# Chunk-band attention layer: third query weight split ahead of the next keys, output copies in the head norm's ring, and sixteen sums moved from GpSimd to VectorE

## The chip, the cores and the metric

The kernel runs on one core of a Trainium2 chip. The metric is device microseconds of one execution, the median of several. The engines are named as the profile names them: PE (TensorE, matrix products; PEld is its weight load), DVE (VectorE), ACT (ScalarE), POOL (GpSimd) and SP (SyncE, which issues most DMAs; SPq is its queue).

## The reference

One inference step of a two-layer trunk over 1024 prompt frames and 8 sample groups of 16 frames, model width 1024. Layer 0 is an RWKV-7 time mixing with an FFN, layer 1 a band attention with an FFN. The change lies in layer 1:

```python
            q = rms_norm((h @ p['wb_q'][j]).reshape(bsz, t, H_B, HEAD_B), p['q_norm'][j])
            o = band_attention(q, k_all, v_all, pos0, k_hist.shape[1], p['rel_bias'][j], qb)
            out = o.reshape(bsz, t, d) @ p['wb_o'][j]
        x = x + gt_m[:, None, :] * out
        h = modulate(rms_norm(x, p['norm_ffn'][l]), sh_f, sc_f)
        x = x + gt_f[:, None, :] * swiglu(h, p['w_gate'][l], p['w_up'][l], p['w_down'][l])
...
    def block(i):                                   # band_attention, 64 queries each
        s = jnp.einsum('bqhd,bkhd->bhqk', q_b, k_b).astype(jnp.float32) * scale + bias[None]
        s = jnp.where(allowed[None, None], s, NEG_INF)
        p = jax.nn.softmax(s, axis=-1)
        return jnp.einsum('bhqk,bkhd->bqhd', p.astype(v_b.dtype), v_b)
```

There are 16 heads of 64; a prompt query sees its own chunk of 64 keys and the 8 chunks before it, a sample query 512 cached keys and its own 16. Queries and keys are normed by head (`q_norm`, `k_norm`).

## The kernel before

**Arithmetic.** Each float32 operand x of a product is split into a high part (`ACTIVATE`, ACT, line 272) and a low part x - high (`TENSOR_TENSOR`, DVE, line 273); `mm3` then issues three matrix products, all at line 143. So a weight is ready for PE when ACT has made its high half and, for the third product, DVE its low half. A weight matrix arrives as two blocks of 128x512 (`halves`, line 249 for the DMA), into raw slots and from there into `wh` tiles of a ring of three.

**Order of the work.** Instructions are written by Python generators, and then put in order on each engine by a scheduler that works from a model of the time; tiles come from pools, each tag a ring of a few buffers, and a tile waits for the last reader of the buffer it takes. `slot(1)` is one such ring, of 128x1024 tiles called `h` in the profile, used for raw weights, raw keys, queries and the splits of FFN inputs. Each engine runs its list in order.

**Stages.** After the keys and values of layer 1, `attention`'s queries for the first two pairs of heads (weights n = 0 and 1) are made with PE fully fed, ending about 2423 us. Then eight pairs of heads are worked through, n = 0 to 7, about 2423 to 2930 us:

- `pair(n)` asks for the keys and queries of the next pair (`kprep`: two DMAs from `out_kT`, line 1624, then a split of 128x1024; `qprep`: a DMA from `qT`, line 1631, then a split of 64x1024 in two parts), the values (`vf`, line 1740) and the bias rows of both heads (`bt`, line 1744, scaled on DVE at 1745).
- 16 tiles, for 8 blocks of 128 queries and two heads, run as a pipeline of four steps: scores on PE (`S<-h,h`) with bias and row minimum on DVE (1802); exponential on ACT (1803); the division on DVE (1805, 1806); transposes of P on PE (1811) and their copy `pts` on ACT (1812); then, for a pair of tiles, the output `O<-pts,vf`. Every second block, `heads_out` copies O (128x256) on DVE (1833) into a tile `o` and sends it to memory.
- Two sample groups per pair (`samples`, cache blocks `kc`, `vc`, queries `qsm`) stand among the tiles.
- As filler, `queries(n + 2)` makes the queries of the pair after the next: `head_steps` issues 24 products `acc<-h,wh` a step group, four groups for each weight, each closed by a head norm: ACT 1518 and 1522, a product `acc<-ht,cst` that sums squares, then `rsqrt2` (ACT 330 to 332, DVE 333, 334) and DVE 1526. Its tiles `ht` come from a ring of five.

Then `attproj` multiplies the outputs by `wo` (about 2931 to 3003 us), eight blocks of weights, adds the residual, and meanwhile makes the FFN's operands of the first half of the frames: `strassen_in` with c = 0 norms X, splits it, and makes sums of blocks (`comb`, line 1299, 128x256 each, 16 of them on POOL) which are split again. The last FFN begins about 3003 us, with the same for the other half (sums on DVE), and keeps PE full from about 3050 us to the end.

The lines that `attention`, `pair` and `attproj` share with the rest:

```python
        self.evt = lambda tag: self.pp.tile([128, 320], F32, tag=tag, ..., bufs={"xin": 2, "ht": 5}[tag])
        gp = gp or nc.gpsimd          # strassen_in(self, B, x, r, A, sh0, c, X, gp=None): engine of the sums
        self.split(t[1], t[2], raw)   # kprep: high part on ACT, low part on DVE
```

Of the kernel before, what the change touches and what calls it, by code (L numbers as in the profile page):

```python
# [8 lines left out]
F32 = mybir.dt.float32  # L9
F32R = mybir.dt.float32r  # L10
AF = mybir.ActivationFunctionType
ALU = mybir.AluOpType
# [133 lines left out]
class Trunk:  # L146
# [133 lines left out]

    def gemm(self, out, W, hi, lo, m=128):

        whi, wlo = W
        for k in range(8):
# [3 lines left out]

    def gemm_steps(self, out, W, hi, lo):

# [1275 lines left out]
    def kv(self, H, X, end):  # L1566
        nc = self.nc
        kn, qn = (self.cp.tile([128, 1], F32, name=n) for n in ("kn2", "qn2"))
        nc.vector.tensor_scalar(kn, self.P("kn", 0), -0.5, None, ALU.mult)
        nc.vector.tensor_scalar(qn, self.P("qn", 0), 0.5 * 0.125, None, ALU.mult)  # L1570
        self.qn = qn
        nw = 4
        W = [self.halves(self.a["wk"][n]) for n in range(nw)]
        for c in (1, 0):
            for n in range(nw):
                self.head(n, c, W[n], H, kn[:, 0:1], self.kT)
                for _ in range(3):
                    next(end, None)
            for _ in end:
                pass  # L1580
        for n in range(nw, 8):
            W = self.halves(self.a["wk"][n])
            for c in (1, 0):
                self.head(n, c, W, H, kn[:, 0:1], self.kT)
        self.HQ = {}
        Aq = self.gain("nm1", 56)
        for n in range(4):
            W = [h for u in range(2) for h in self.halves(self.a["wv"][n, u])]
            for c in range(2):
                for w in range((4, 5)[c]):  # L1590
                    ws = slice(w * 128, (w + 1) * 128)
                    pz = self.wide()[:, 0:256]
                    for k in range(8):
                        ks = slice(k % 2 * 256, (k % 2 + 1) * 256)
                        wh, wl = W[k // 2]
                        self.mm3(pz, H[c][0][k][:, ws], H[c][1][k][:, ws], wh[:, ks], wl[:, ks], k == 0, k == 7)
                    vt = self.ev("vt")[:, 0:256]
                    nc.scalar.activation(vt, pz, AF.Copy)
                    nc.sync.dma_start(self.o["v"][4 * c + w, :, n * 256:(n + 1) * 256], vt)
                if n == 3:  # L1600
                    self.HQ[c] = self.feats(c, F32R), self.feats(c, F32R)
                    for _ in self.normed_split(c, *X[c], Aq, 48, *self.HQ[c]):
                        pass
        self.KQ = {}
        for e in range(2):
            self.kprep(0, e)
        for n in range(2):
            if n:
                self.evt = lambda tag: self.slot(1)
            W = self.halves(self.a["wq"][n])  # L1610
            for c in range(2):
                self.head(n, c, W, self.HQ, qn[:, 0:1], self.qT)
            if n == 0:
                for e in range(2):
                    self.qprep(0, e)
# [18 lines left out]
    def attention(self, ctx):  # L1634
        nc, tc = self.nc, self.tc
        at = self.at = self.pp = self.wq = ctx.enter_context(tc.tile_pool(name="att", bufs=1, reuse_waits="tile"))
        self.hw = ("wh", "wl", 3)
        self.halfraw = lambda: self.slot(1)[:, :512]
        self.evt = lambda tag: self.pp.tile([128, 320], F32, tag=tag, name=self.nm(tag), bufs={"xin": 2, "ht": 5}[tag])
        self.qbd = at.tile([128, 4, 2, 16], F32, name="qbd")  # L1640
        nc.gpsimd.memset(self.qbd, 0.0)
        self.X, self.xs = {}, {}
        self.O = self.bank("O", 1)
        self.flow = [None] * 3
        for n in range(8):
            if n < 6:
                self.qgen = self.queries(n + 2)
                next(self.qgen, None)
            self.qn_ = 2 if n < 6 else 3
            self.pair(n)  # L1650
            if n < 6:
                for _ in self.qgen:
                    pass
        for _ in self.qgen:
            pass
        rest = self.proj_rest()
        next(rest)
        for _ in range(3):
            self.advance(None)
        return rest  # L1660
# [59 lines left out]
    def queries(self, n):  # L1720

        nc = self.nc
        W = self.halves(self.a["wq"][n])
        yield
        for c, o, m in ((0, 0, 256), (0, 256, 256), (1, 0, 320), (1, 320, 320)):
            yield from self.head_steps(n, c, o, m, W, self.HQ, self.qn[:, 0:1], self.qT)
# [7 lines left out]
    def pair(self, n):  # L1734
        nc = self.nc
        if n < 7:
            self.kprep(n + 1, 0)
            self.qprep(n + 1, 0)
        vf = self.att("vf", [128, 8, 128], 2)
        nc.sync.dma_start(vf, self.o["v"][0:8, :, n * 128:(n + 1) * 128].rearrange("w p d -> p w d"))  # L1740
        bias = []
        for e in range(2):
            bt = self.att("bt", [128, 641], 3)
            nc.sync.dma_start(bt, self.a["rel"][2 * n + e])
            nc.vector.tensor_scalar(bt[:, 384:640], bt[:, 384:640], bt[:, 640:641], -1.0, ALU.subtract, ALU.mult)
            bias.append(bt)
        order = [(e, qt) for qt in range(8) for e in range(2)]
        groups = self.samples(n)
        for i, (e, qt) in enumerate(order):
            self.advance(self.tile(n, qt, e, vf, bias[e]))  # L1750
            if n == 6 and i in (4, 5, 6, 8, 9, 10):
                self.xprep(*divmod((4, 5, 6, 8, 9, 10).index(i), 3))
                if i == (4, 5, 6, 8, 9, 10)[2]:
                    self.qgen = self.proj_part()
            if n == 7 and i in (4, 5):
                self.xprep(i - 4, 3)
            if (e, qt) == (0, 7) and n < 7:
                self.kprep(n + 1, 1)
                self.qprep(n + 1, 1)
            if i in (1, 9):  # L1760
                self.advance(next(groups))
# [65 lines left out]
    def heads_out(self, n, t0, O):  # L1827

        nc = self.nc
        w = O.shape[-1]  # L1830
        if n < 7:
            o = self.att("o", [128, 256], 1)
            nc.vector.tensor_copy(o[:, 0:w], O)
            nc.sync.dma_start(self.og[n, :, t0:t0 + w], o[:, 0:w])
            return
        c = t0 // 512 if t0 < 1024 else 1
        s = slice(t0 - 512 * c, t0 - 512 * c + w)
        self.split(self.X[c][0][7][:, s], self.X[c][1][7][:, s], O)
# [71 lines left out]
    def attproj(self, B, x2, x3, rest):  # L1910

        nc = self.nc
        tags = {"kk": ("pts", 2), "x": ("P", 3), "o": ("P", 3)}
        self.evt = lambda tag: self.at.tile([128, 640], F32, tag=tags.get(tag, tags["kk"])[0], name=self.nm(tag), bufs=tags.get(tag, tags["kk"])[1])
        self.halfraw = lambda: self.att("vf", [128, 8, 128], 2).rearrange("p a b -> p (a b)")[:, :512]
        A = self.gain("nf1", 80)
        r = self.sq_done(next(rest))
        t = [self.slot(1)[:, :1024] for _ in range(4)]
        sub = self.strassen_in(B, x3, r, A, 72, 0, [t[k // 2][:, k % 2 * 512:(k % 2 + 1) * 512] for k in range(8)])
        st = self.sq_open()  # L1920
        st.acc = self.rs[:, 640:1280]
        for n in range(8):
            W = self.halves(self.a["wo"][n])
            d, parts = self.pz(1)
            for z, o, m in parts:
                for k in range(8):
                    wh, wl = W[k // 4]
                    s = slice(k % 4 * 128, (k % 4 + 1) * 128)
                    hi, lo = (self.X[1][h][k][:, o:o + m] for h in range(2))
                    self.mm3(z, wh[:, s], wl[:, s], hi, lo, k == 0, k == 7)  # L1930
            x, o = (self.ev(t) for t in "xo")
            nc.sync.dma_start(x, x2[:, n, self.cols(1)])
            self.residual(512, n, 64, o, x, d)
            nc.sync.dma_start(x3[:, n, self.cols(1)], o)
            if n == 0:
                nc.scalar.activation(st.acc, o, AF.Square)
            else:
                self.sq_add(st, o)
            next(sub, None)
        for _ in sub:  # L1940
            pass
        return A, st
# [43 lines left out]
```

## Time and profile before

| | before |
|---|---|
| time, median of 3 runs | 3811.97 us (3804.54 to 3815.72) |
| the profiled execution's own time | 3804.49 us |
| its span | 3802.7 us |
| instructions | 72100 |
| mean granted PE clock | 0.940 |
| PE busy | 3506.1 us (92%) |
| DVE busy | 2263.6 us (60%) |
| ACT busy | 1573.8 us (41%) |
| POOL busy | 591.6 us (16%) |
| DMA | 554.01 MB, mean 146 GB/s |

The profile is of one execution. In its rows, a group is given by line, engine, operation and tiles (output<-inputs), and brackets at a row's end tell how long the engine stood idle before it and which operation released it. The clock is the share of full speed that PE was granted in a stretch.

### The profile page before, as it was taken

How to read it: one execution, taken by the hardware profiler on the slowest of the kernel's cores; microseconds unless marked ns; L12 is line 12 of the kernel's file. 1: busy time of each engine (PE TensorE's matmuls, PEld its weight loads, DVE VectorE, ACT ScalarE, POOL GpSimd, SP SyncE). 2: the span in 40 equal slices, each digit the busy share in tenths (PEclk: the TensorE clock that was granted, in tenths of full speed). 3: DMA queues.
4: the chain of work that ended last, by engine and by line, in shares of the span. 5: the costliest groups of instructions: out<-in, count | busy, mean ns of one | idle time of the engine just before them, and what ended most of it. 6: DMA issues, size and time to landing. Idle time of an engine off the chain costs nothing.

```text
span 3802.7 us, 72100 instructions
## 1 busy us (share of the span) xinstructions
PE 3506.1 (92%) x28550; PEld 3098.0 (81%) x28550; DVE 2263.6 (60%) x4396; ACT 1573.8 (41%) x3006; POOL 591.6 (16%) x497
## 2 busy tenths in 40 slices
PE   5889989989999799999999899789889799999999
PEld 4777778777667699999888879667677799999898
DVE  4666667765445854554457742666565755545667
ACT  5545546544223533333311452556554533333310
POOL 0000000000011154453000100000000255444000
PEclk9887899899699899999999999899899899999999
DMA  5876776776665322224654122554565322222521
GB/s 212 236 216 170 207 220 184 201 203 201 192 197 176 113 84 76 76 73 157 221 177 172 64 71 92 153 151 155 152 203 178 120 78 71 76 75 96 171 86 66
DMA packets 426995, 554.01 MB, mean 146 GB/s; under 512 B 128385, under 2 KB 292737, under 8 KB 422177
## 3 DMA queue, kind: packets, MB, share of 16 engines
q1 hardware_dynamic: 351344, 450.68, 36.9%
q0 software_dynamic: 22224, 80.36, 6.9%
q10 hardware_dynamic: 53088, 18.36, 2.1%
q8 instruction: 225, 3.69, 0.4%
q14 instruction: 114, 0.93, 0.1%
HBM read 415.85 MB, written 133.40 MB: 144 GB/s over the span
## 4 chain that ended last, share of the span: by engine, by line
PE 69%; DMA 11%; DVE 10%; issue 4%; ACT 4%; SPq 1%; ACTq 0%; POOL 0%; DVEq 0%; POOLq 0%
PE S L143 32%; PE PT L143 15%; PE acc L143 12%; PE st L143 3%; PE O L143 2%; PE G L143 1%; DVE h L273 1%; PE aux L143 1%; PE PT L1811 1%; PE Y L143 1%; DMA TT<-Z 1%; DMA h<-out_kT 1%; DVE wlo L273 1%; DMA raw<-in_rw_o 1%; DMA h<-in_wo 1%
## 5 line engine op out<-in xcount | busy, mean ns | idle before, releaser
L143 PE MATMUL S<-h,w 128*128 128x320 f32 (+1 forms) x4944 | 689.7, 298 | 12.3 <-ACT h L272 4.8
L143 PEld LDWEIGHTS S<-h,w 128*128 128x128 f32 x4944 | 671.8, 191 | 18.4 <-ACT h L272 5.6
L143 PE MATMUL S<-h,wh 128*128 128x320 f32 (+1 forms) x2844 | 529.8, 338 | 15.9 <-DVE h L1170 6.8
L143 PE MATMUL acc<-mx,whi 128*128 128x384 f32 x1728 | 508.5, 372 | 32.7 <-ACT whi L272 13.0
L143 PEld LDWEIGHTS S<-h,wh 128*128 128x128 f32 x2844 | 456.1, 189 | 70.8 <-issue 12.3
L272 ACT ACTIVATE w<-rq 128x512 fp32r<-128x512 f32 x308 | 192.6, 629 | 515.1 <-PE S L143 201.1
L143 PEld LDWEIGHTS acc<-mx,whi 128*128 128x128 f32 x1728 | 337.6, 204 | 63.3 <-ACT whi L272 16.9
L273 DVE TENSOR_TENSOR w<-rq,w 128x512 fp32r<-128x512 f32 x308 | 267.8, 872 | 199.8 <-ACT w L272 199.0
L143 PE MATMUL PT<-h,w 128*128 128x320 f32 (+1 forms) x2448 | 347.6, 297 | 10.2 <-ACT h L272 4.7
L143 PEld LDWEIGHTS PT<-h,w 128*128 128x128 f32 x2448 | 332.1, 190 | 12.2 <-ACT h L272 5.1
L143 PE MATMUL acc<-mx,wlo 128*128 128x384 f32 x864 | 316.1, 366 | 8.3 <-DVE wlo L273 8.3
L1369 POOL TENSOR_TENSOR t<-t,t 128x576 f32<-128x576 f32 (+1 forms) x132 | 226.5, 1717 | 442.2 <-ACT t L1376 320.1
L143 PE MATMUL PT<-h,wh 128*128 128x320 f32 (+1 forms) x1428 | 284.2, 342 | 8.2 <-ACT h L1558 2.3
L143 PEld LDWEIGHTS PT<-h,wh 128*128 128x128 f32 x1428 | 231.7, 188 | 38.5 <-issue 5.0
L143 PEld LDWEIGHTS acc<-mx,wlo 128*128 128x128 f32 x864 | 175.0, 203 | 20.6 <-DVE wlo L273 12.9
L273 DVE TENSOR_TENSOR wlo<-raw,whi 128x1024 fp32r<-128x1024 f32 x114 | 139.1, 1221 | 84.9 <-ACT whi L272 83.8
L272 ACT ACTIVATE wh<-rq 128x512 fp32r<-128x512 f32 x124 | 74.8, 625 | 245.1 <-PE S L143 161.4
L273 DVE TENSOR_TENSOR h<-h,h 128x1024 fp32r<-128x1024 f32 (+4 forms) x112 | 122.3, 1106 | 88.3 <-ACT h L272 72.1
L272 ACT ACTIVATE whi<-raw 128x1024 fp32r<-128x1024 f32 x114 | 119.6, 1053 | 129.0 <-PE acc L143 62.6
L272 ACT ACTIVATE h<-h 128x1024 fp32r<-128x1024 f32 (+4 forms) x112 | 103.5, 935 | 159.8 <-DMA h<-sd 111.1
L1369 DVE TENSOR_TENSOR t<-S,t 128x576 f32<-128x576 f32 (+1 forms) x116 | 86.4, 744 | 122.7 <-PE S L143 122.7
L1436 DVE TENSOR_TENSOR h<-h,S 128x640 f32<-128x640 f32 (+1 forms) x150 | 111.9, 750 | 78.9 <-PE S L143 78.7
(444 smaller groups left out, 5625.0 us busy)
## 6 DMA issues: line engine op xcount, KB each, us to landing
h<-in_wada SPq DMA_DIRECT2D x64, 512.0 KB, 6.3
rq<-in_wg SPq DMA_DIRECT2D x88, 256.0 KB, 2.6
rq<-in_wu SPq DMA_DIRECT2D x88, 256.0 KB, 2.6
rq<-in_wd SPq DMA_DIRECT2D x88, 256.0 KB, 3.1
raw<-in_wada POOLq DMA_DIRECT2D x32, 512.0 KB, 5.0
kc<-in_ck SPq DMA_DIRECT2D x16, 1024.0 KB, 5.1
vc<-in_cv SPq DMA_DIRECT2D x16, 1024.0 KB, 6.0
sd<-t SPq DMA_DIRECT2D x88, 160.0 KB, 1.9
```

The lines of the kernel that those rows point to most:

```text
L143: return nc.tensor.matmul(out, lhsT, rhs, start=start, stop=stop)
L272: self.nc.scalar.activation(hi, x, AF.Copy)
L273: self.nc.vector.tensor_tensor(lo, x, hi, ALU.subtract)
L1369: eng.tensor_tensor(out, x, y, ALU.add)
L1436: nc.vector.tensor_tensor(y, y, d, ALU.add)
L1811: nc.tensor.transpose(pt[:, j * 128:(j + 1) * 128], P[:, j * 128:(j + 1) * 128], self.C("ident"))
```

## The change

1. The raw weight of the third pair (n = 2) is fetched by one DMA of 128x1024 when the second weight's queries begin, into a `slot(1)` tile; `queries(2)` splits it in two halves, without a DMA of its own. The first `pair`'s `kprep` and `qprep` are put under `issue_after`, that is behind the second half's high part in the order.
2. The output copies of `heads_out` take a tile of the head norm's ring `ht`, which has six buffers in place of five; the tile `o` is gone.
3. The sums of `strassen_in` for c = 0 in `attproj` go to DVE.

```diff
@@ -1606,6 +1606,8 @@
             if n:
+                self.q2 = self.slot(1)[:, :1024]
+                nc.sync.dma_start(self.q2, self.a["wq"][2])
                 self.evt = lambda tag: self.slot(1)
@@ -1636,7 +1638,7 @@
-        self.evt = lambda tag: self.pp.tile([128, 320], F32, tag=tag, name=self.nm(tag), bufs={"xin": 2, "ht": 5}[tag])
+        self.evt = lambda tag: self.pp.tile([128, 320], F32, tag=tag, name=self.nm(tag), bufs={"xin": 2, "ht": 6}[tag])
@@ -1720,7 +1722,15 @@
-        W = self.halves(self.a["wq"][n])
+        if n == 2:
+            W = []
+            for p in range(2):
+                W.append([self.wq.tile([128, 512], F32R, tag=t, name=self.nm("wh"), bufs=3) for t in ("wh", "wl")])
+                raw = self.q2[:, p * 512:(p + 1) * 512]
+                self.q2_split = nc.scalar.activation(W[p][0], raw, AF.Copy)
+                nc.vector.tensor_tensor(W[p][1], raw, W[p][0], ALU.subtract)
+        else:
+            W = self.halves(self.a["wq"][n])
         yield
@@ -1734,8 +1744,9 @@
         if n < 7:
-            self.kprep(n + 1, 0)
-            self.qprep(n + 1, 0)
+            with self.tc.issue_after(self.q2_split.ins):
+                self.kprep(n + 1, 0)
+                self.qprep(n + 1, 0)
@@ -1829,7 +1840,7 @@
-            o = self.att("o", [128, 256], 1)
+            o = self.ev("ht")
@@ -1916,7 +1927,7 @@
-        sub = self.strassen_in(B, x3, r, A, 72, 0, [t[k // 2][:, k % 2 * 512:(k % 2 + 1) * 512] for k in range(8)])
+        sub = self.strassen_in(B, x3, r, A, 72, 0, [t[k // 2][:, k % 2 * 512:(k % 2 + 1) * 512] for k in range(8)], nc.vector)
```

The lists of the engines differ from about 2407 us on, where the new weight's DMA stands. Lines behind 1610 have moved up to 11 lines further down in the changed file (1624 is 1626, 1631 is 1633, 1740 is 1751, 1744 is 1755, 1811 is 1822, 1844 is 1855). Three places follow.

SP at the attention's opening, before. `h` tiles of `in_wq` at line 249 are the third weight, of `out_kT` the next keys, `h<-qT` at 1631 queries to be split, `qT<-rq` finished queries of the second weight on their way to memory:

```order
L1631 DMA h_25125<-qT 64x1024
L1631 DMA h_25129<-qT 64x1024
L249 DMA h_25270<-in_wq 128x512
L1538 DMA qT<-rq_25170 128x512
L249 DMA h_25276<-in_wq 128x512
L1624 DMA h_25285<-out_kT 64x1024 x2
L1538 DMA qT<-rq_25209 128x320
L1538 DMA qT<-rq_25248 128x320
L1740 DMA vf_25294<-out_v 128x8x128
L1631 DMA h_25290<-qT 64x1024
L1744 DMA bt_25296<-in_rel 128x641
L1844 DMA qsm_25337<-qT 128x128
```

SP at the same place, now:

```order
L1633 DMA h_25125<-qT 64x1024
L1633 DMA h_25129<-qT 64x1024
L1610 DMA h_25133<-in_wq 128x1024
L1538 DMA qT<-rq_25172 128x512
L1626 DMA h_25283<-out_kT 64x1024 x2
L1538 DMA qT<-rq_25211 128x320
L1538 DMA qT<-rq_25250 128x320
L1751 DMA vf_25292<-out_v 128x8x128
L1755 DMA bt_25294<-in_rel 128x641
L1855 DMA qsm_25335<-qT 128x128
L1633 DMA h_25288<-qT 64x1024
```

The weight comes by one DMA in front of the query writes, and the bias rows and the sample queries stand ahead of the next pair's queries.

PE in the first half of pair n = 1, where a tile of three key blocks is transposed (other pairs have the same pattern), before. `acc_26257` is the filler, 21 products in all here, and the next transpose (`PT_26265`) stands behind them:

```order
L143 MATMUL S_26305<-h_25894,h_25893 128x256
L143 MATMUL S_26305<-h_25895,h_25893 128x256
L1811 MATMUL PT_26227<-cst,P_26182 128x128 x3
L143 MATMUL O_25269<-pts_26196,vf_25948 64x128
L143 MATMUL acc_26257<-h_24892,wh_25926 128x320
L143 MATMUL acc_26257<-h_24896,wh_25926 128x320
L143 MATMUL acc_26257<-h_24892,wh_25927 128x320
```

PE at the same tile, now; `acc<-ht,cst` is the head norm's sum of squares:

```order
L143 MATMUL S_26303<-h_25892,h_25891 128x256
L143 MATMUL S_26303<-h_25893,h_25891 128x256
L1822 MATMUL PT_26225<-cst,P_26180 128x128 x3
L143 MATMUL O_25271<-pts_26194,vf_25946 64x128
L143 MATMUL acc_26243<-ht_26244,cst 128x256
L1822 MATMUL PT_26263<-cst,P_26203 128x128 x4
L143 MATMUL O_25271<-pts_26224,vf_25946 64x128
L143 MATMUL O_25271<-pts_26194,vf_25946 64x128
```

Before, the norm's sum of squares stood ahead of the first transposes of this half; now it stands here, and the filler comes three transposes later, 24 products in one piece.

DVE in the projection, before. `wh<-vf,wh` is the low half of a projection weight, `h<-h,h` at line 273 the low half of an FFN operand:

```order
L273 TENSOR_TENSOR wh_31408<-vf_31405,wh_31407 128x512
L273 TENSOR_TENSOR h_31119<-h_31037,h_31118 128x256
L1175 TENSOR_TENSOR o_31297<-o_31297,x_31296 128x128
L273 TENSOR_TENSOR h_31119<-h_31037,h_31118 128x256
L311 TENSOR_TENSOR h_30893<-h_30893,kk_31303 128x640
L273 TENSOR_TENSOR h_31119<-h_31038,h_31118 128x256
L273 TENSOR_TENSOR h_31121<-h_31037,h_31120 128x256
L273 TENSOR_TENSOR h_31123<-h_31039,h_31122 128x256 x2
L273 TENSOR_TENSOR h_31123<-h_31040,h_31122 128x256 x2
L273 TENSOR_TENSOR h_31119<-h_31038,h_31118 128x256
L273 TENSOR_TENSOR wh_31414<-vf_31411,wh_31413 128x512
```

DVE at the same place, now:

```order
L273 TENSOR_TENSOR wh_31406<-vf_31403,wh_31405 128x512
L1299 TENSOR_TENSOR h_31036<-h_31036 128x256 x2
L1299 TENSOR_TENSOR h_31035<-h_31035,h_31037 128x256
L273 TENSOR_TENSOR h_31117<-h_31035,h_31116 128x256
L1175 TENSOR_TENSOR o_31295<-o_31295,x_31294 128x128
L1299 TENSOR_TENSOR h_31035<-h_31035,h_31037 128x256
L273 TENSOR_TENSOR h_31117<-h_31035,h_31116 128x256
L1299 TENSOR_TENSOR h_31036<-h_31036,h_31038 128x256 x2
L273 TENSOR_TENSOR h_31117<-h_31036,h_31116 128x256
L1299 TENSOR_TENSOR h_31037<-h_31037,h_31035 128x256
L273 TENSOR_TENSOR h_31117<-h_31036,h_31116 128x256
L273 TENSOR_TENSOR wh_31412<-vf_31409,wh_31411 128x512
```

Between two low halves of weights stand seven sums and four low halves of operands, where there were nine low halves; six more sums stand ahead of this piece.

## The prediction

> **What bounds the kernel now.** I read the page first (busy times and chain), then busy time and clock by stretch from the place where the two kernels part, then the waits of TensorE (PE) there, then the timeline of the three stretches where PE is not full.
>
> ```profile
> PE 3506.1 (92%) x28550; PEld 3098.0 (81%) x28550; DVE 2263.6 (60%) x4396; ACT 1573.8 (41%) x3006; POOL 591.6 (16%) x497
> PE 69%; DMA 11%; DVE 10%; issue 4%; ACT 4%; SPq 1%; ACTq 0%; POOL 0%; DVEq 0%; POOLq 0%
> ```
>
> PE is the bound, 92% busy and 69% of the chain. No matmul is removed, so only PE's idle time and its time at half clock can be saved. The two orders are the same on every engine up to about 2407 us; what follows is where the change can act. In the next rows the columns are the stretch, its length, busy us of PE, weight loads, DVE, ACT and POOL, then granted clock, DMA share and GB/s.
>
> ```profile
> 2400.00:2450.00 50.00, 34.82 (x164) 27.17 (x165) 22.27 (x51) 20.81 (x46) 0.00 (x0) 0.71 0.63 191
> 2950.00:3000.00 50.00, 42.49 (x267) 41.71 (x268) 33.86 (x64) 20.57 (x45) 16.20 (x16) 0.90 0.36 120
> 3000.00:3050.00 50.00, 33.90 (x174) 29.86 (x173) 43.77 (x104) 28.60 (x59) 9.63 (x4) 0.80 0.30 107
> 3050.00:3100.00 50.00, 49.98 (x375) 49.92 (x376) 31.65 (x41) 18.97 (x33) 29.10 (x20) 1.00 0.27 88
> ```
>
> PE stands for 15.2, 7.5 and 16.1 us in the first three, and from 3050 on it is full: nothing later can give or take. Between them lies the attention, where PE's waits from 2440 to 2930 us that the change can touch are (total, times, longest):
>
> ```profile
> PE acc L143 <- ACT ht L1522: 5.7, 6, 1.5
> PE acc L143 <- DVE ht L333: 5.1, 3, 3.2
> PE O L143 <- DVE o L1833: 4.4, 2, 2.3
> ```
>
> **A: the third query weight.** Timeline of the attention's opening, with the one large wait of SyncE's queue:
>
> ```profile
> SPq L249 <- DVE h L334: 9.3, 1, 9.3
> 2408.39 1.10 SPq L1631 DMA_DIRECT2D h<-qT  x2
> 2420.70 1.12 SPq L1624 DMA_DIRECT2D h<-out_kT  x2
> 2420.76 0.47 ACT L332 ACTIVATE h<-h 128x320 f32<-128x320 f32 x1
> 2422.65 0.55 DVE L1526 SCALAR_TENSOR_TENSOR rq<-rq,qn,h 128x320 f32<-128x320 f32 x1
> 2426.17 1.06 ACT L272 ACTIVATE h<-h 128x1024 fp32r<-128x1024 f32 x1 [4.93 <-DMA h<-out_kT]
> 2426.75 0.46 SPq L1631 DMA_DIRECT2D h<-qT  x1
> 2427.13 1.13 ACT L272 ACTIVATE wh<-h 128x512 fp32r<-128x512 f32 x2
> 2427.79 0.80 PE L143 MATMUL acc<-h,wh 128*128 128x256 f32 x2 [8.13 <-ACT wh L272]
> 2429.14 5.06 PE L143 MATMUL acc<-h,wh 128*128 128x256 f32 x22 [0.55 <-DVE wh L273]
> 2431.22 0.35 DVE L1745 TENSOR_SCALAR bt<-bt 128x256 f32<-128x256 f32 x1 [1.53 <-DMA bt<-in_rel]
> 2434.74 0.37 ACT L1518 ACTIVATE xin<-acc 128x256 f32<-128x256 f32 x1
> 2434.80 0.47 PE L1811 MATMUL PT<-cst,P 128*128 128x128 f32 x1 [0.60 <-DVE P L1806]
> 2439.80 4.42 PE L143 MATMUL acc<-h,wh 128*128 128x256 f32 x19 [1.30 <-DVE ht L333]
> ```
>
> Before, SyncE stands 9.3 us for a slot that the head norm holds, and ACT, idle 4.93 us for the next keys, splits them ahead of the weight. After, one DMA of 1024 columns replaces two of 512 and stands right behind the pair at 2408.39, so it is issued near 2409.5; the keys took 5.5 us from issue (2420.70) to their split (2426.17), so it lands near 2415, while the norm runs. One DMA fewer is issued; nothing new waits on SyncE, since the slot it takes is free by then. ACT splits behind its last L332 (2420.76 + 0.47 = 2421.2, first half done 2421.8) and DVE behind its last L1526 (2422.65 + 0.55 = 2423.2, first half done 2423.9). The high products start at about 2421.9, the low ones at 2423.9 in place of 2429.14: 5.2 us early. That is not yet the gain, for then the first tile of attention is late: its bias, scaled at 2431.22, waits for a DMA that SyncE issues behind the query load at 2426.75. In the new order the bias stands ahead of that load, and right behind the values: issued 3.1 us earlier, so scaled near 2428.1. The first P comes near 2431.1 (DVE's copies of the sample queries, which stand between, wait for the query writes as before), and the transpose at 2431.1 in place of 2434.80. The keys' split, now behind the weight's (issue_after puts it there), loses nothing: it lands no earlier than 2425 and its ACT is free by 2422.5. The weight's query head closes by ACT L1518 (2434.74), now behind two exponentials and the query split, near 2432.4, and the norm after it releases PE's next lump near 2437.4 in place of 2439.80. **Term A: −2.4 us.** It can't be a loss by these rows unless the keys come late (end 0); the other end is the clock, which is half throughout:
>
> ```profile
> 2430.00:2437.00 7.00, 6.04 (x25) 4.90 (x25) 4.06 (x15) 3.11 (x9) 0.00 (x0) 0.50 0.65 202
> 2437.00:2443.30 6.30, 5.00 (x20) 3.95 (x20) 1.33 (x3) 1.31 (x3) 0.00 (x0) 0.50 1.02 330
> 2550.99 2.85 PE L143 MATMUL acc<-h,wh 128*128 128x256 f32 x22
> ```
>
> PE was 6.04 of 7 us busy in the first row and still had half clock in the second. If a start without the 8.13 us gap returned the clock earlier, the 19 products of 4.42 us would take 19/22 of 2.85, 2.5 us (−1.9), and the transposes and scores up to 2443.30 as much again: end −6. I keep the half clock, since these rows show it surviving a busy stretch.
> The Trainium skill ("TensorE: Matmul & The Clock Gate", Part 1: The HAM clock gate) says that the clock is halved after an idle window of about 3.4 us and restored after one of sustained work, which would have restored it near 2433 here; the trace does not agree, it shows 0.50 to 2443.3. By the rule term A would be near its end of −6.
>
> **B: the attention.** Copies of outputs move from a scratch of their own (one buffer) to the ring of the head norm (six in place of five): 28 copies of 256 columns and 7 of the samples, as many as before and as many DMAs. The new order is another list for all eight pairs. Halves of pairs, from one sample group's end to the next:
>
> ```profile
> 2483.38:2516.56 33.18, 26.13 (x233) 20.37 (x232) 19.53 (x57) 17.44 (x43) 0.00 (x0) 0.95 0.53 155
> 2575.05:2603.06 28.01, 26.37 (x235) 21.68 (x234) 17.99 (x53) 17.60 (x40) 0.00 (x0) 1.00 0.37 121
> 2603.06:2630.78 27.72, 24.28 (x234) 18.98 (x233) 18.56 (x57) 17.07 (x43) 0.00 (x0) 1.00 0.68 203
> 2782.84:2807.60 24.76, 18.69 (x185) 12.95 (x184) 16.09 (x53) 15.97 (x37) 0.00 (x0) 1.00 0.82 282
> 2556.76 0.43 PE L143 MATMUL O<-pts,vf 128*64 128x128 f32 x2 [2.12 <-DVE o L1833]
> ```
>
> In the halves of the kind of the second row PE is idle 1.64 us. There the new order takes the filler (query products) out of the first five tiles and puts it behind the sixth (the lines of PE in the section on the change): what an uncovered tile costs shows in the last half, with no filler: 6.07 us idle over 8 tiles and a sample group, 0.67 each. Six uncovered tiles give 4.0 us idle, so a half can lose 2.4 us, and at least 0 if the later lumps still cover; my walk down the new order gives +1.7, nearer the uncovered row. Six such halves: +10. Against it stand the waits for L1522, L333 and the output copy, 5.7 + 5.1 + 4.4 = 15.2 us. The norm's sum now stands behind another tile's transpose and output, so its inputs have a tile more time, and with a ring of six the copy is not held by one buffer; I take four fifths, −12. **Term B: −2 us**, between +12 (filler lost, few waits gone) and −12 (the reverse). The DVE copy can't get cheaper or dearer: same 256 columns. The ring's release is the copy's DMA in place of the norm's last read, but with six slots no row shows anyone waiting for it.
>
> **C: the projection's sums.**
>
> ```profile
> L1299 DVE TENSOR_TENSOR x<-x,x x36: 411/475/482, 1257.6 to 3047.7; 128x320 f32<-128x320 f32 x24, 128x256 f32<-128x256 f32 x12
> 2953.72 2.77 DVE L273 TENSOR_TENSOR h<-h,h 128x256 fp32r<-128x256 f32 x8
> 2955.28 4.98 POOL L1299 TENSOR_TENSOR h<-h,h 128x256 f32<-128x256 f32 x3 [574.60 <-DVE h L273]
> 2965.38 6.10 POOL L1299 TENSOR_TENSOR h<-h,h 128x256 f32<-128x256 f32 x7
> 2955.94 8.94 PE L143 MATMUL S<-h,wh 128*128 128x320 f32 x58
> 2966.70 0.56 PE L143 MATMUL S<-h,wh 128*128 128x320 f32 x2 [1.82 <-ACT wh L272]
> 2970.82 1.21 DVE L273 TENSOR_TENSOR wh<-vf,wh 128x512 fp32r<-128x512 f32 x1
> 2972.08 7.81 PE L143 MATMUL S<-h,wh 128*128 128x320 f32 x34 [4.82 <-DVE wh L273]
> ```
>
> Sixteen sums of 128x256 run on POOL from 2955.28 to 2971.48, at 0.87 us each at the end; ACT's and DVE's splits of them go at that pace, and the next weight's low half (2970.82) is queued behind them on DVE. PE waits 1.82 + 4.82 = 6.64 us, then runs 34 products in 7.81 us. On DVE a sum of 256 columns takes 0.41 us (least of the first row). Down the new order, from 2956.5 (2953.72 + 2.77, the first splits' end) to that low half: 13 sums and 4 low halves at 0.41 are 7.0 us, and the seven other operations that stand there as before are some 3.5 (half a microsecond each): done near 2967.7 in place of 2972.0. PE is there at about 2964.9 (2955.94 + 8.94) and meets smaller waits on the way, so I leave it 2.0 of the 6.64 us. Without the long stall the 34 products run at full clock, in 5.2 us by the rate of the 58 ahead of them: −2.6. **Term C: −6.64 + 2.0 − 2.6 = −7.2 us**; ends −4 (clock not kept, more left of the stall) and −8.5 (0.7 left of it). DVE is 6.6 us busier in a stretch where it had the time.
>
> **D: the opening of the last FFN.** Its first weights' splits move behind the normed input's second half.
>
> ```profile
> 3018.05 2.50 PE L143 MATMUL PT<-h,w 128*128 128x256 f32 x10 [3.10 <-DVE w L273]
> ```
>
> PE then gets its first two groups early and the third (3018.05) near 3025, but with all inputs there. Its idle time stays near 16 us, since DVE, which paces the stage, has the same work and is as full as before (43.77 of 50). I take +1, between −2 and +4.
>
> **Sum:** −2.4 − 2 − 7.2 + 1 = −10.6 us. The profiled execution took 3804.49 us, which becomes 3793.9; it is the fastest of the times shown, so against the median of 3811.97 I say 3801.4. About 0.3% (11.4 us) is what a measurement of this kernel can tell from no change, and the forecast lies just inside it.
>
> **Rivals.** (1) The attention keeps the filler's cover and loses its waits: B = −12, sum −20.6, 3791. For it: the waits are named; against: the lumps do move. (2) The clock returns early at the opening: A = −6, sum −14.2, 3798; the half clock at 6.04 of 7 us busy speaks against. (3) The projection's stall moves to DVE: C near 0, since the sums push every low half back as much as POOL's pace did; sum −3.4, 3809. DVE's 33.86 of 50 us speaks against. (4) The ring doesn't relieve the waits (the norm, not the buffer, was late) and the filler is lost in six halves: B = +10, sum +1.4, 3813. (5) Slower: both kinds of half lose the cover of their tiles, 13 halves at +1.7 and no wait goes: B = +22, sum +13.5, 3825. It decides from about +1.5 a half. The 24.76 us half, 76% busy, shows that tiles alone can't fill PE; the second kind's large lumps of filler, which remain, speak against.
>
> **Chances.** Forecast 0.45 (own range 3796 to 3806, 0.20 of it beyond the bound), (1) 0.15, (2) 0.10, (3) 0.12, (4) 0.08, (5) 0.10. Faster 0.20 + 0.15 + 0.10 = 0.45; same 0.25 + 0.12 + 0.08 = 0.45; slower 0.10. Range 3787 to 3817: it leaves out (5) and some 0.07 below.
>
> **What the changed profile would show.** A: PE's wait of 8.1 us for ACT's wh gone, first transpose near 2431; clock by stretch tells (2). B: no wait for an output copy, halves of the first kind near 29.7 us, the second under 30; total length of the attention within 12 us. C: no POOL work at 2955, PE's wait for wh under 2 us, clock 1.00 through 2975. D: PE idle 14 to 20 us from 3000 to 3050. I am wrong if the attention's length moves by more than all else, which the unequal halves make possible.

## The result and the profile after

The change made the kernel slower: 3832.76 us (median) against 3812.43 us, ratio 1.0054 with a 95% interval of 1.004 to 1.0069. The forecast was 3801.4 us in a range of 3787 to 3817, so the time lies outside it, on the other side. The profiled execution took 3825.66 us with a span of 3823.6, against 3804.49 and 3802.7. One of the changed kernel's thirteen executions took 13245.92 us; it counts in the median and not in the ratio.

The page of the changed kernel, its busy times and chain, first:

```profile
PE 3511.1 (92%) x28550; PEld 3097.4 (81%) x28550; DVE 2268.1 (59%) x4412; ACT 1574.7 (41%) x3006; POOL 567.0 (15%) x481
PE 19%; DVE 2%; DMA 0%; issue 0%; ACT 0%; SPq 0%; DVEq 0%; ACTq 0%
```

The same 28550 products, and the sixteen sums gone from POOL (481 instructions for 497) to DVE (4412 for 4396). The second row is cut short: the chain was followed back only part of the way here, so it can't be laid beside the one of before.

To find where the 20.9 us of span went I cut both traces at the same instructions: the product of the head norm that closes the first part of the second weight's queries, the transposes that end the first and the last of the sixteen sample groups (`PT<-cst,xin`), and the first product of the last FFN's norm (`PT<-h,cst`). The rows of the attention and the projection, by stretch (length, busy PE, weight loads, DVE, ACT, POOL, clock, DMA share, GB/s), before, then after:

```profile
2455.46:2898.05 442.59, 391.64 (x3476) 313.71 (x3474) 281.48 (x814) 259.09 (x592) 0.00 (x0) 0.96 0.52 163
2898.05:3004.15 106.10, 92.57 (x608) 85.43 (x609) 66.69 (x121) 45.01 (x87) 16.20 (x16) 0.95 0.47 153
```

```profile
2456.48:2925.81 469.33, 408.84 (x3475) 323.82 (x3473) 289.34 (x814) 259.38 (x593) 0.00 (x0) 0.93 0.50 154
2925.81:3024.87 99.06, 89.98 (x609) 82.89 (x609) 65.90 (x137) 44.58 (x87) 0.00 (x0) 1.00 0.50 162
```

| stretch | before | after | difference | forecast |
|---|---|---|---|---|
| up to the norm's product | 2414.11 | 2418.86 | +4.75 | 0 |
| opening, to the first group's end | 41.35 | 37.62 | -3.7 | -2.4 |
| attention, first to last group's end | 442.59 | 469.33 | +26.7 | -2 |
| projection, to the FFN's norm | 106.10 | 99.06 | -7.0 | -7.2 |
| the rest | 798.6 | 798.7 | +0.2 | +1 |

The first row is no effect of the change: the shift is there ahead of the first instruction that differs (the pair of query loads that is issued at 2408.39 before is issued at 2413.03 now, 4.6 us later, and the new weight's load only behind it, at 2414.17), and other executions with the same list up to there differ by as much (2412.02 to 2434.01 in the kernels below). All of the loss is in the attention. Its two rows show two parts: the same products keep PE busy 17.2 us longer (408.84 against 391.64), at a mean clock of 0.93 for 0.96, and PE stands 9.5 us longer (60.5 for 50.95).

PE's longest waits there in the changed kernel:

```profile
PE PT L1822 <- DVE so L1917: 17.3, 14, 2.6
PE PT L1822 <- ACT pts L1823: 13.3, 23, 1.3
PE PT L1822 <- ACT pts L1901: 10.9, 5, 2.8
PE PT L143 <- ACT pts L1823: 4.9, 3, 3.3
PE acc L143 <- DVE ht L333: 4.9, 5, 1.0
PE PT L1913 <- DVE xin L1911: 3.1, 3, 2.2
PE O L143 <- DVE ht L1844: 0.2, 1, 0.2
```

and the two of before that answer to the first and third:

```profile
PE PT L1811 <- DVE so L1906: 5.8, 11, 0.7
PE PT L1811 <- ACT pts L1890: 0.5, 1, 0.5
```

The wait for the output copy is gone, as forecast (4.4 us, now 0.2). In its place PE waits for `so`, the two copies of 64x64 that take a sample group's output out of the PT bank, which all transposes share, and for `pts L1901`, the copy of the group's own transposes out of the same bank. What has changed is what PE has to do meanwhile. Before, behind a group's last transpose (all engines but SP, weight loads left out):

```profile
2575.05 0.27 PE L1902 MATMUL PT<-cst,xin 128*128 128x128 f32 x1
2575.16 0.60 PE L143 MATMUL acc<-ht,cst 128*128 128x256 f32 x2
2575.25 0.70 DVE L1802 CUSTOM_DVE_ANT_0 S<-S,bt 128x512 f32<-128x512 f32 x1 [0.66 <-PE S L143]
...
2575.87 0.45 DVE L1906 COPY so<-PT 64x64 f32<-64x64 f32 x2
2576.46 0.41 PE L1811 MATMUL PT<-cst,P 128*128 128x128 f32 x2 [0.71 <-DVE so L1906]
```

After:

```profile
2611.16 0.27 PE L1913 MATMUL PT<-cst,xin 128*128 128x128 f32 x1
...
2611.59 1.23 DVE L273 TENSOR_TENSOR h<-h,h 128x1024 fp32r<-128x1024 f32 x1 [1.74 <-ACT h L272]
2612.73 0.82 DVE L1813 CUSTOM_DVE_ANT_0 S<-S,bt 128x640 f32<-128x640 f32 x1
2613.47 0.14 DVE L1813 DVE_READ_ACCUMULATOR2_ANT st<- 128x1 f32 x1
2613.47 0.45 DVE L1917 COPY so<-PT 64x64 f32<-64x64 f32 x2
2613.96 0.23 DVE L1844 COPY ht<-so 128x128 f32<-128x128 f32 x1
2614.07 1.30 PE L1822 MATMUL PT<-cst,P 128*128 128x128 f32 x5 [2.64 <-DVE so L1917]
```

The norm's product `acc<-ht,cst` no longer stands between the two transposes, and on DVE the copies stand behind the low half of the next keys and a row of scores: PE stands 2.64 us for 0.45 us of copying, the longest of the 14 such waits. Where only the scores are ahead it is 1.14 us, for 0.71 before. The clock follows. The same five columns in stretches of 2 us, behind another group's end (2519.30):

```profile
2518.00:2520.00 2.00, 1.57 (x16) 0.97 (x14) 0.85 (x2) 0.39 (x1) 0.00 (x0) 1.00 0.81 183
2520.00:2522.00 2.00, 0.75 (x4) 0.54 (x5) 0.56 (x4) 0.78 (x2) 0.00 (x0) 0.95 0.93 377
2522.00:2524.00 2.00, 2.00 (x11) 1.34 (x10) 1.09 (x4) 1.76 (x6) 0.00 (x0) 0.50 0.18 65
2524.00:2526.00 2.00, 2.00 (x12) 1.83 (x11) 1.13 (x4) 0.00 (x1) 0.00 (x0) 0.70 0.19 66
2526.00:2528.00 2.00, 2.00 (x19) 1.54 (x18) 1.45 (x5) 1.90 (x5) 0.00 (x0) 1.00 0.00 0
```

Counted in such stretches between the first and the last group's end, the clock is cut 14 times in the changed kernel and 6 times before; seven of the 14 begin within 4 us of a group's end.

### The profile page after: what moved, and what is told of

It is laid out like the page before. It is cut to its first block, busy times and chain, and to the rows that moved or that the text cites. A ratio compares the mean times of both kernels' runs of the same rounds, so it can differ in the third digit from the quotient of the medians.

```text
span 3823.6 us, 72079 instructions
## 1 busy us (share of the span) xinstructions
PE 3511.1 (92%) x28550; PEld 3097.4 (81%) x28550; DVE 2268.1 (59%) x4412; ACT 1574.7 (41%) x3006; POOL 567.0 (15%) x481
## 5 line engine op out<-in xcount | busy, mean ns | idle before, releaser
L143 PEld LDWEIGHTS acc<-mx,whi 128*128 128x128 f32 x1728 | 336.7, 203 | 63.3 <-ACT whi L272 16.9
L143 PE MATMUL PT<-h,w 128*128 128x320 f32 (+1 forms) x2448 | 346.7, 297 | 14.2 <-ACT w L272 7.4
```

Of the source, the lines that this page charges most:

```text
L143: return nc.tensor.matmul(out, lhsT, rhs, start=start, stop=stop)
```

## The experiments

All times below are ratios to the kernel before, run on the same chip at the same time, with 95% intervals; "attention" is the stretch of the table, 442.6 us before and 469.3 after. It comes from one execution of each kernel, and in the eight kernels that keep the old pattern on PE it lies between 436.7 and 446.3 us, so a difference of less than some 10 us between two traces tells little by itself.

**Each part alone, and the change without one.** Output copies in the ring alone (part 2 of the change):

```diff
-        ... bufs={"xin": 2, "ht": 5}[tag])
+        ... bufs={"xin": 2, "ht": 6}[tag])
-            o = self.att("o", [128, 256], 1)
+            o = self.ev("ht")
```

> Only the output copies in the head norm's ring, six buffers. Theory R: sharing this ring is what rewrites the list of the attention, and the list costs the time: the attention (first sample group's end to last) is about 25 us longer than before as in the changed kernel, opening and projection as before, so 3812 + 25 = about 3837 us, slower than the whole change. Theory Q (the early third weight and issue_after shift the loads of keys and queries, and that costs): within 5 us of before. Theory S (sums on VectorE cost): within 5 us of before.

Measured: 1.0061 (1.0045 to 1.0077), slower. Attention 462.5 us, clock 0.95; waits for `so` 18.1 us in 14, for the group's `pts` 10.2 us in 5: the changed kernel's pattern. PE's list shows it without a run: written as T for a tile's transposes, H for the norm's product and A for filler, the first half of a pair begins `H T T`, with 21 A behind the third T, in the kernel before and `T T .. T O H T`, with 24 A behind the sixth, here. With five slots in the ring (the run with three buffers of `xin` below), or six, this part of the list is the same; so it is the sharing and not the size.

The third weight alone (part 1):

```diff
+                self.q2 = self.slot(1)[:, :1024]
+                nc.sync.dma_start(self.q2, self.a["wq"][2])
...
+            with self.tc.issue_after(self.q2_split.ins):
```

> Only the third query weight loaded and split early, with issue_after. Theory R: first transpose of the attention 3.5 us earlier, the attention's list nearly as before, so 2 to 3 us faster than before, which is too little to be told by the time, and is read from the trace. Theory Q: slower than before by 10 us or more, in the attention. Theory S: as R.

Measured: 0.9993 (0.9981 to 1.0006), no change that can be told, centre -2.7 us. Attention 436.7 us.

The sums alone (part 3, `nc.vector` as last argument of `strassen_in`):

> Only the sixteen sums of the projection on VectorE. Theory R: attention unchanged, wait for the low half of the weight under 1 us, projection 5 to 7 us shorter, so about 3806 us. Theory S: the sums push the low halves back and the time is the same or longer, 3812 to 3818 us. Theory Q: as R.

Measured: 0.9981 (0.9967 to 0.9996), centre -7.2 us. From the last group's end to the FFN's norm it takes 99.07 us for 106.10 before.

Parts 1 and 3 together, the ring and its five buffers as before:

> The changed kernel with the output copies in their own scratch and a ring of five again. Theory R: all the gain without the loss, 8 to 10 us faster than before, 3802 to 3804 us, some 28 us faster than the whole change. Theory Q: slower than before by 10 us. Theory S: as before or slower.

Measured: 0.9989 (0.9974 to 1.0003). The centre is -4.2 us, less than the 8 to 10 us that I expected and than the 10 us of the parts, whose sum the interval just reaches. Theory R stands: with the ring the kernel is slower by 0.5 to 0.6%, without it at least as fast as before. Theories Q and S fall.

**What in the new list costs.** The copies `so` on ScalarE, in the changed kernel:

```diff
-            nc.vector.tensor_copy(so[h, 4 * g:4 * g + 4, :], pv[h, :, e, :])
+            nc.scalar.activation(so[h, 4 * g:4 * g + 4, :], pv[h, :, e, :], AF.Copy)
```

> The changed kernel with the two copies that end a sample group (so, 64x64 each) on ScalarE in place of VectorE; TensorE's list is the same but for the last two pairs. Theory P: the new list leaves nothing between the sample group's last transpose and the next tile's, so that TensorE waits there for copies that stand behind other work on VectorE (17.3 us in 14 waits); with them on ScalarE that wait falls under 8 us and the attention is 8 to 12 us shorter than in the changed kernel, about 3822 us. Theory X (the loss comes from ScalarE, blocked by the two buffers of xin): the copies queue behind the same blocked engine, no gain or up to 5 us worse, 3832 to 3838 us.

Measured: 1.0022 (1.0007 to 1.0037): some 12 us of the loss are gone, as theory P had it. But not by the path it gave (the attention by stretch, PE's wait, and one such wait in the timeline):

```profile
2462.37:2917.52 455.15, 399.56 (x3475) 318.48 (x3473) 282.57 (x784) 265.50 (x623) 0.00 (x0) 0.95 0.52 159
```

```profile
PE PT L1822 <- ACT so L1917: 15.2, 14, 2.2
```

```profile
2587.22 0.44 PE L1822 MATMUL PT<-cst,P 128*128 128x128 f32 x2 [0.54 <-ACT so L1917]
```

The attention is 14.2 us shorter, yet the wait fell only from 17.3 to 15.2 us, not under 8. It was halved in the first halves of pairs (1.14 to 0.54 us, last row), where ACT is free, and grew in some of the second ones, where ACT is behind (1.75 us at one place for 1.27). Of the 14.2 us, 9.3 are busy time of the same products (399.56 for 408.84), which goes with the clock: nine cuts in place of 14. The six first halves are 175.1 us for 182.9, none of them holding a cut, and the last three halves 96.8 for 103.9, with another list on PE in part of them; the second halves gain nothing.

Three buffers of `xin` and five of `ht`:

```diff
+        ... bufs={"xin": 3, "ht": 5}[tag])
```

> The changed kernel with three buffers of xin and five of ht in the place of two and six; TensorE's list is the same but in the last pair. Theory X: ScalarE's waits at L1518 for a query write (18.3 us in 4) go, TensorE's waits for pts L1901 (10.9 us) fall under 5, the attention is 6 to 10 us shorter, about 3825 us. Theory P: ScalarE's waits are mostly idle time that costs nothing; the attention within 4 us of the changed kernel, 3829 to 3836 us.

Measured: 1.0057 (1.0041 to 1.0073); attention 470.9 us. ACT's waits at L1518 for a query's write (18.3 us in 4) did go, and nothing came of it: PE's waits for `so` and `pts L1901` stayed (16.9 and 9.9 us). ACT was early there, not late: at L1518 it now waits for PE's `acc` instead (53.2 us in 21). Theory X falls.

Work for PE in the gap:

```diff
+        for _ in range(5):
+            mm(nc, pt[:, 512:640], self.C("ident"), self.C("ident"), True, True)
```

> The changed kernel with five useless products of 128x128 by 128 behind the last transpose of each sample group, into a part of the PT bank that nobody reads: TensorE computes where it stands waiting for the copies so (17.3 us in 14). Its list is the same but for the last two pairs. 16 x 5 products at about 0.2 us add 16 us of work, nearly all inside the waits. Theory C (a stall of 1 to 3 us at a sample group's end costs mostly by the half clock that follows it): half-clock stretches that begin at a group's end vanish, the real work is done at a higher clock, and the time falls by 4 to 10 us in spite of the added work: 3820 to 3826 us. Rival I (what counts is the standing time itself): the products hide in the wait or lengthen it, clock unchanged, 3830 to 3840 us.

Measured: 1.0067 (1.005 to 1.0083), a median of 3838.84 us, where rival I had put it; theory C's forecast is wrong. The attention is 483.3 us, but in the slowest of the six executions (3860.74 us). The useless products write the tile that the copies read, the copies waited for them too, and the wait grew to 19.7 us:

```profile
2500.34 0.27 PE L1913 MATMUL PT<-cst,xin 128*128 128x128 f32 x1
2500.44 1.28 PE L143 MATMUL PT<-cst 128*128 128x128 f32 x10
2503.37 0.74 PE L1822 MATMUL PT<-cst,P 128*128 128x128 f32 x5 [1.65 <-DVE so L1919]
```

The first halves of the first five pairs were all 30.3 to 30.4 us, where in the changed kernel they are 29.7 in two and 31.2 to 32.0 in three, so the cuts behind these ends did vanish; in the second halves they stayed, and the sixth first half has one (33.0 us). Whether the clock could be bought this way without the longer wait is open.

**Looking for a better kernel.** Two buffers of `o` of its own and four of `ht`, in the kernel before:

> The kernel before with two buffers of o in place of one and four of ht in place of five. Theory R (sharing the ring rewrites the list): list as before, TensorE's wait for the copy (4.4 us) gone, 0 to 5 us faster, 3806 to 3811 us. Rival: any relief of the output copy lets the tiles run ahead and rewrites the attention, 3830 us.

Measured: 1.0019 (1.0006 to 1.0032), slightly slower, so that neither forecast of the time was met: the list on PE is nearly that of before, the wait for the copy is gone from it, and there is no gain, for the norm's waits stayed (5.6 us for L1522, 5.0 for L333) and the one for `pts` grew to 23.7. So the 4.4 us were no price to be had back. With the same edit, parts 1 and 3:

> Early third weight, sums on VectorE, and output copies in two buffers of their own with four of ht: Theory R: sum of the parts, 3811 - 2.5 - 7 - 3 = about 3799 us, clear of no change. Rival: the parts don't add, since the lists differ between them (their union alone gave -4), 3805 to 3809 us.

Measured: 1.0004 (0.999 to 1.0018); the rival was nearer. Parts 1 and 3 with the copies `so` on ScalarE, and part 3 with them:

> Early third weight and sums on VectorE, output copies as before in their own scratch, and the copies so on ScalarE. Theory P: in the list of before TensorE waits 5.8 us for these copies; with them earlier, 2 to 4 us less on top of the union's gain, about 3801 us. Rival (the copies delay the exponentials and pts on ScalarE): 3808 us or more.

> The sums on VectorE and the copies so on ScalarE, third weight and output copies as before. Theory P: 3804 - 3 = about 3801 us. Rival: 3808 us or more.

Measured: 0.9983 (0.9972 to 0.9993) and 0.9995 (0.9981 to 1.0008). Theory P's 3801 us was met by neither (3804.92 and 3809.96); the second lies where its rival put it. The first and the sums alone (0.9981) are the fastest kernels of the study, both under the 0.3% that I called tellable, and clear of 1 by their intervals.

## Why the prediction was wrong

**A held in its events.** Shifted by the 4.75 us that lie ahead, the forecast events came where the order put them: high products at 2426.56 - 4.75 = 2421.8 (2421.9 forecast), low ones 2423.9 (2423.9), the bias 2428.7 (2428.1), the first transpose 2431.3 (2431.1), the next lump 2437.2 (2437.4).

```profile
2426.56 0.79 PE L143 MATMUL acc<-h,wh 128*128 128x256 f32 x2 [2.14 <-DVE h L333]
2428.61 4.83 PE L143 MATMUL acc<-h,wh 128*128 128x256 f32 x22 [1.26 <-DVE wh L1731]
2433.41 0.35 DVE L1756 TENSOR_SCALAR bt<-bt 128x256 f32<-128x256 f32 x1 [1.54 <-DMA bt<-in_rel]
2436.02 0.33 PE L1822 MATMUL PT<-cst,P 128*128 128x128 f32 x1 [2.57 <-DVE P L1817]
2441.93 4.85 PE L143 MATMUL acc<-h,wh 128*128 128x256 f32 x21 [1.30 <-DVE ht L333]
```

The 8.13 us wait became 2.14. The clock did come back early, from 2433.05 to 2436.47, but in most of that time PE stood for the first P, and for the lump of 4.85 us it was at half again; so rival (2) fell. The size can't be told from the opening's length: it fell by 3.7 us here, by 1.7 with the early weight alone, and by 3.1 with the sums alone, whose opening is unchanged. Where the prediction says that the half clock up to 2443.3 speaks against a return after sustained work, it misread the trace: on the grid of 3.41 us described in the last section, PE was busy for 0.89 of a stretch at most there, until one from 2441.89 on was full, and behind that one the clock came back.

**C held**, to 0.2 us: 16 sums in the time that DVE had, PE's wait for the weight's low half 0.7 us, clock 1.00 through the stage. From the last group's end to the FFN's norm the four kernels with the sums on POOL take 105.3 to 107.5 us, and seven of the nine with the sums on DVE 98.5 to 100.0 (the other two, 103.1 and 105.9, with a clock below 1.00). Rival (3) fell. **D** was +0.2 for +1.

```profile
PE S L143 <- DVE wh L273: 0.7, 1, 0.7
```

**B failed:** +26.7 us, outside both ends I gave (+12 and -12). Four steps of it are to blame, by kinds of halves (sums over the stretches between groups' ends, before and after):

| | before | after |
|---|---|---|
| first halves (6) | 170.0 | 182.9 |
| second halves (6) | 182.2 | 182.5 |
| last three, with the projection as filler | 90.5 | 103.9 |

1. First halves, +13 for the +10 forecast. The walk was right at full clock: 29.7 us, just what I had written. I carried it at the clock of the rows it was walked from, 1.00, and three of the six fell to half clock for 3.4 us behind a group's end.
2. Second halves: I credited four fifths of the three named waits, -12. The copy's wait did go, and so did the waits for L1522, while the one for L333 moved to the first halves (5.0 us there); but the waits for `so` (9.1 us for 1.3) and for the group's `pts` (10.9 for 0.5) came in their place. PE stands there 29.1 us for 32.4, a gain of 3.3 in place of 12, and products at a lower clock took 3.6 us more, so these halves gained nothing. The step that failed is "what is late next": the named releaser ends a wait, and PT, with one buffer, ends the next. The run with two buffers of `o` shows the same thing on the old list.
3. The last pair, whose filler is the projection, I left out altogether, as I priced only the halves whose filler are queries. It cost 13.4 us, half of the whole (8.0 us, 98.5 for 90.5, in the one execution with the ring alone). Its list is another too, and PE's busy time there grew from 81.2 to 89.8 us. Which entry of that list costs it is not settled; putting `so` on ScalarE brought 7.1 us of it back, with the list of the last pairs changed again.
4. I took the clock as a thing of the opening (rival (2)) and of the projection's long stall. Of the +26.7 us, 17.2 are the same products at a lower clock.

Rival (5), slower by 13 halves at +1.7 us, named the sign and the order of the time (3825) with a chance of 0.10, but not the mechanism: the loss is not 1.7 us in each of 13 halves. The second halves lost 0.3 us in all, one of them 8.1 (27.7 to 35.8, at a clock of 0.81 for 1.00) while the other five gained. Rival (4) came nearest to the cause, little relief and the filler's place lost in six halves; its +10 for B lacks the clock and the last three halves.

What stays open is why sharing the ring makes the scheduler write the other list. The ring itself is no wait on the chip: in the changed kernel no engine stands for a buffer of `ht` that a copy's write to memory still holds. The runs show only that the list comes with the sharing, at five buffers and at six.

## What to carry to other kernels

When a scheduler orders the work, a change of buffers is a change of the list for every stage that uses them: price it from the order of each stage, the odd ones at the end too, before the wait that it removes. Ask of each bank with one buffer what PE has to do between the last write and the copy out; a product that stands there hides the copy, and its moving away costs the wait and, at times, the clock behind it. Try such parts apart: here a part that gains 7 us, and one with -2.7 that can't be told from no change, hid under one that loses 23.

## What the runs showed of the hardware

**Short stalls cut the clock.** The rows at 2518 to 2528 above: PE stands 1.14 and 0.54 us within two microseconds, and the clock is then at half for 3.4 us though PE is full. The same waits, to 0.02 us, behind the group's end at 2581.42 cut nothing, and that half took 29.74 us for 32.04. The three first halves with such a cut took 1.5 to 2.3 us more than the two of 29.7 us. The trace shows what decides: every change of the clock in it, as in the other kernels' traces, falls on one grid of 3.41 us that runs through the whole execution. Cut along that grid (columns as before), the two places are

```profile
2518.39:2521.80 3.41, 1.73 (x11) 1.12 (x11) 1.39 (x5) 0.96 (x3) 0.00 (x0) 1.00 0.86 279
2521.80:2525.22 3.42, 3.42 (x15) 2.76 (x15) 1.44 (x5) 1.97 (x6) 0.00 (x0) 0.50 0.25 91
2579.83:2583.24 3.41, 2.27 (x16) 1.66 (x15) 1.05 (x4) 0.38 (x1) 0.00 (x0) 1.00 0.69 272
2583.24:2586.65 3.41, 2.88 (x22) 2.37 (x22) 2.06 (x7) 2.49 (x7) 0.00 (x0) 1.00 0.06 18
```

Behind 2519.30 both waits fall into one stretch, PE is busy 1.73 of its 3.41 us, and the next stretch has half clock. Behind 2581.42 the grid parts the two waits, and nothing is cut. In the changed kernel's attention all 14 stretches at full clock with PE busy for a share of 0.56 or less are followed by half clock, and none with 0.63 or more is; the clock comes back only behind a stretch with 0.97 or more. In the kernel before, the two kinds overlap a little (cut up to 0.61, spared from 0.55).
The Trainium skill ("TensorE: Matmul & The Clock Gate", HAM oscillation — how this bites in real kernels) puts the rule as no idle gaps of PE above about 3.4 us. The trace doesn't agree as far as that threshold goes: no single gap here is longer than 1.14 us. That page's Part 1: The HAM clock gate says that the window is free-running, which lets the same stall count in one place and not in another; the trace agrees, by its grid of 3.41 us.

**Sums on GpSimd cost VectorE as much as doing them.** DVE's sixteen sums of 0.41 us add 6.6 us of work to the projection, yet its busy time there is 65.90 us for 66.69 (rows of the first section). Its low halves, while POOL adds (before) and with the sums on DVE (after; minimum, median and maximum in ns):

```profile
L273 DVE TENSOR_TENSOR h<-h,h x15: 405/545/947, 2954.7 to 2972.8; 128x256 fp32r<-128x256 f32 x15
L273 DVE TENSOR_TENSOR wh<-vf,wh x3: 686/1054/1209, 2957.1 to 2970.8; 128x512 fp32r<-128x512 f32 x3
```

```profile
L273 DVE TENSOR_TENSOR h<-h,h x16: 411/416/418, 2983.7 to 2999.8; 128x256 fp32r<-128x256 f32 x16
L273 DVE TENSOR_TENSOR wh<-vf,wh x4: 680/682/682, 2986.1 to 2998.2; 128x512 fp32r<-128x512 f32 x4
```

The Trainium skill ("SBUF — State Buffer", SBUF: two separate sides) says that a VectorE operation with two SBUF inputs and GpSimd exclude each other at a shared port, for a whole instruction. These rows agree: operations of 0.41 us take up to 0.95 beside POOL, and 0.42 at most without it.
